# Scaled a and r of an RWKV-7 recurrence interleaved in their scratch, and its identity blocks copied on chip

## The chip, the cores and the metric

The kernel runs on one core of a Trainium2 chip. The metric is the device time of one execution in microseconds (us). The engines are TensorE (PE, matmuls and transposes), VectorE (DVE), ScalarE (ACT), GpSimd (POOL) and SyncE (SP, whose queue issues most transfers). Each engine works through its own list of instructions in order, and semaphores tie the lists together.

## What is computed

The reference is a trunk of two layers on 512 tokens of width 1024 in float32. Layer 0 mixes tokens by RWKV-7, layer 1 by a spatial gating unit, and each is followed by a SwiGLU feed-forward layer. The change lies in layer 0, in the recurrence of 16 heads of width 64:

```python
def step(S, inp):
    r_t, w_t, k_t, v_t, a_t, b_t = inp
    sa = jnp.einsum('bhij,bhj->bhi', S, a_t)
    S = (S * w_t[:, :, None, :]
         + sa[..., None] * b_t[:, :, None, :]
         + v_t[..., None] * k_t[:, :, None, :])
    y = jnp.einsum('bhij,bhj->bhi', S, r_t)
    return S, y
```

## The kernel before, in words

The recurrence isn't stepped token by token. The sequence is cut into 8 chunks of 64 tokens (C = 64, NC = 8), and what happens inside a chunk is solved for all chunks beforehand, so that only 8 short steps per head remain in sequence. The 16 heads are handled in 4 blocks b of 4 heads: in a block, q (0, 1) picks a pair of heads, and the two heads hd of a pair lie in the upper and the lower 64 partitions. hh (0, 1) picks a half of the chunks, and cc one of its 4 chunks.

The work of layer 0 is a list of steps, `PLAN` (line 33). For block b they are:

- **P**, `kr_proj`: the k and r projections. A weight unit of 512 KB comes by SP's queue (line 138), ScalarE rounds it to a high part (131), VectorE makes the low part (132), and TensorE does three products for each (`mm3`, 156 to 158).
- **E**, `early`: decay, keys and the scaled operands. `ma` is the scaled a (it lies in the buffer of tw), and r is scaled in place (656, 668). Both are written to DRAM scratch `sa` (670, 671), and k and kp to scratch `sb` (674), already interleaved by chunk. Scratch is there because the next step wants other partitions and another order. The buffers of tw and ta come from a pool of two, so ScalarE's first write to the next block's tw (619) waits until the transfer of `sa` has read the old one.
- **V**, `v_proj`: the values, in four steps of two weight units each, thus eight units of 48 products for all heads.
- **F**, `front`: loads from scratch. `ST` takes 512 KB of `sb` (682). For each of the four units (hh, q) the tile `MV` holds a and r block-diagonally by head: GpSimd clears the other half (687) and transfers bring a and r (689), n = 0 for a and 1 for r. The tile `BX` gets identity blocks by transfers from the constant `ident` (702), into `bx[head, 2 + hd]`. Then TensorE multiplies `MV` by `ST` (`lm`, 708) and transposes `ST` (`bkt`, 721). VectorE writes masked products into `MV` and `BX` (711, 716), and ScalarE fills `LA` and `BX` (714, 715, 725, 726).
- **B**, `back`: the triangular solve. VectorE transposes `LA` (734), runs 15 dependent pairs of small operations (747, 749) and transposes the result twice (752, 753). TensorE then joins the parts in a chain of small products (`Qp`, `Np`, `Tp`, `Q2p`, `T2p`, 769 to 801), `mp` (810) and `gh` (817). VectorE adds the identity blocks of `BX` to `gh` and writes the chunk operators into `MV` (819, 820). `mvt` (760) are transposes of `MV` that `mp` needs.
- **S**, `scan`: the 8 chunks in sequence: `us` (846) and `Yp` (859) on TensorE, the state update on VectorE and ScalarE (848, 851), the values by SP (831).
- **N**, `finish`: group norm, bonus and gate.

The plan is only the order in which the instructions are written. A scheduler with a timeline of its own then orders every engine's list, so any edit can move instructions far from its place. `MV`, `BX`, the split inputs `xsp` and others share one pool of 17 slots (tag s); four of the inputs of V lie there until V's last product. A `BX` copy thus waits for a slot, and so does what stands behind it on its queue. All waits of a transfer are taken on the queue that issues it, in order.

## Time and profile before

| what | value |
|---|---|
| median of 3 runs | 1393.85 us (1392.23 to 1398.0) |
| profiled execution | 1395.72 us |
| its span, first to last instruction | 1394.0 us |
| mean granted clock of TensorE | 0.971 |
| busy time of TensorE, VectorE, ScalarE, GpSimd | 1332.0, 783.9, 579.2, 152.6 us |
| transfers of `sa` into `MV` (689) | 64 of 64 KB |
| transfers of `ident` into `BX` (702) | 32 of 64 KB |
| writes of `sa` (670, 671) | 8 of 512 KB |

Rows of groups have the form "line engine operation out<-in xcount". A busy TensorE isn't TensorE at its peak: its clock is granted by a throttle, and a stretch at 0.5 takes twice the time for the same work. Rows marked SPq are issues of transfers: their time is that of the issue, not of the transfer.

### The profile page before, as it was taken

How to read it: one execution, taken by the hardware profiler on the slowest of the kernel's cores; microseconds unless marked ns; L12 is line 12 of the kernel's file. 1: busy time of each engine (PE TensorE's matmuls, PEld its weight loads, DVE VectorE, ACT ScalarE, POOL GpSimd, SP SyncE). 2: the span in 40 equal slices, each digit the busy share in tenths (PEclk: the TensorE clock that was granted, in tenths of full speed). 3: DMA queues.
4: the chain of work that ended last, by engine and by line, in shares of the span. 5: the costliest groups of instructions: out<-in, count | busy, mean ns of one | idle time of the engine just before them, and what ended most of it. 6: DMA issues, size and time to landing. Idle time of an engine off the chain costs nothing.

```text
span 1394.0 us, 21544 instructions
## 1 busy us (share of the span) xinstructions
PE 1332.0 (96%) x8512; PEld 1088.7 (78%) x8512; DVE 783.9 (56%) x1373; ACT 579.2 (42%) x1076; POOL 152.6 (11%) x190
## 2 busy tenths in 40 slices
PE   5999979989799899999999999999999999999998
PEld 3677768878687688888888887878888888888886
DVE  7975776579847565544553225575574554453223
ACT  5665765566543453222322224543463332232121
POOL 5000200111000021111110002010121111110000
PEclk8999979989799999999999999999999999999999
DMA  5145375432214233333322332342223333332231
GB/s 150 36 140 148 108 208 166 127 77 69 92 49 158 61 101 112 91 95 102 91 91 91 103 109 76 107 138 89 91 77 93 103 91 93 103 92 91 91 105 61
DMA packets 209956, 142.00 MB, mean 102 GB/s; under 512 B 59536, under 2 KB 185024, under 8 KB 209856
## 3 DMA queue, kind: packets, MB, share of 16 engines
q1 hardware_dynamic: 208560, 135.91, 33.0%
q0 software_dynamic: 1296, 4.72, 1.0%
q8 instruction: 67, 1.10, 0.3%
q14 instruction: 33, 0.27, 0.1%
HBM read 124.35 MB, written 14.16 MB: 99 GB/s over the span
## 4 chain that ended last, share of the span: by engine, by line
PE 62%; DVE 2%; ACT 0%; issue 0%; DVEq 0%
PE gu L157 12%; PE gu L158 12%; PE gu L156 11%; PE acc L157 8%; PE acc L158 8%; PE acc L156 8%; PE u L158 1%; PE u L157 1%; PE u L156 1%; DVE x L273 1%; PE s L1065 1%; PE ptr L218 0%; DVE hT L59 0%; DVE rt L208 0%; DVE ry L209 0%; DVE hn L270 0%
## 5 line engine op out<-in xcount | busy, mean ns | idle before, releaser
L131 ACT CAST whi<-wraw 128x1024 fp32r<-128x1024 f32 x177 | 185.7, 1049 | 481.3 <-PE gu L157 250.5
L132 DVE TENSOR_TENSOR wlo<-wraw,whi 128x1024 fp32r<-128x1024 f32 x177 | 263.1, 1487 | 206.3 <-ACT whi L131 202.3
L156 PE MATMUL gu<-hT,whi 128*128 128x512 f32 (+1 forms) x768 | 288.8, 378 | 1.8 <-ACT hT L57 1.7
L157 PE MATMUL gu<-hT,whi 128*128 128x512 f32 (+1 forms) x768 | 288.5, 377 | 1.1 <-DVE hT L59 1.1
L158 PE MATMUL gu<-hT,wlo 128*128 128x512 f32 (+1 forms) x768 | 289.5, 378 | 0.0
L156 PEld LDWEIGHTS gu<-hT,whi 128*128 128x128 f32 x768 | 145.0, 190 | 31.5 <-ACT hT L57 2.3
L157 PEld LDWEIGHTS gu<-hT,whi 128*128 128x128 f32 x768 | 144.9, 189 | 30.5 <-DVE hT L59 1.5
L158 PEld LDWEIGHTS gu<-hT,wlo 128*128 128x128 f32 x768 | 145.1, 189 | 28.5 <-issue 0.2
L157 PE MATMUL acc<-wlo,act 128*128 128x512 f32 x416 | 164.0, 394 | 0.0
L156 PE MATMUL acc<-whi,act 128*128 128x512 f32 x416 | 163.5, 394 | 0.0
L158 PE MATMUL acc<-whi,act 128*128 128x512 f32 x416 | 160.4, 394 | 0.0
L332 DVE TENSOR_TENSOR sg<-sg,gu 128x512 f32<-128x512 f32 x44 | 30.3, 688 | 142.2 <-PE gu L158 139.2
L333 POOL TENSOR_TENSOR sg<-sg,hn 128x512 f32<-128x512 f32 x44 | 57.0, 1295 | 417.3 <-DVE sg L332 417.3
L156 PEld LDWEIGHTS acc<-whi,act 128*128 128x128 f32 x416 | 78.2, 188 | 18.1
L158 PEld LDWEIGHTS acc<-whi,act 128*128 128x128 f32 x416 | 78.2, 188 | 18.0
L157 PEld LDWEIGHTS acc<-wlo,act 128*128 128x128 f32 x416 | 78.1, 188 | 18.0
L330 DVE TENSOR_TENSOR sg<-gu,hn 128x512 f32<-128x512 f32 x44 | 30.4, 691 | 66.5 <-PE gu L158 66.3
L131 ACT CAST act<-sg 128x512 fp32r<-128x512 f32 x52 | 32.3, 621 | 71.7 <-POOL sg L333 57.5
L156 PE MATMUL proj<-xsp,whi 128*128 128x512 f32 x128 | 51.6, 403 | 0.0
L158 PE MATMUL proj<-xsp,wlo 128*128 128x512 f32 x128 | 51.1, 401 | 0.0
L157 PE MATMUL proj<-xsp,whi 128*128 128x512 f32 x128 | 50.3, 396 | 0.2 <-DVE xsp L132 0.2
L708 PE MATMUL lm<-MV,ST 128*128 128x128 f32 x256 | 40.0, 309 | 7.0 <-ACT BX L726 3.0
(303 smaller groups left out, 2124.0 us busy)
## 6 DMA issues: line engine op xcount, KB each, us to landing
wraw<-in_ffn_w_gate_dram SPq DMA_DIRECT2D x44, 512.0 KB
wraw<-in_ffn_w_up_dram SPq DMA_DIRECT2D x44, 512.0 KB, 3.8
wraw<-in_ffn_w_down_dram SPq DMA_DIRECT2D x44, 512.0 KB, 3.7
wraw<-in_rwkv_w_rkv_dram SPq DMA_DIRECT2D x24, 512.0 KB, 3.7
wraw<-in_sgu_w_in_dram SPq DMA_DIRECT2D x16, 512.0 KB, 3.7
x<-in_x_dram SPq DMA_DIRECT2D x8, 512.0 KB, 3.2
MV<-sa SPq DMA_DIRECT2D x64, 64.0 KB, 2.5
ST<-sb SPq DMA_DIRECT2D x8, 512.0 KB
```

The source lines that it names most:

```text
L131: self.nc.scalar.copy(hi, src)
L132: self.nc.vector.tensor_tensor(lo, src, hi.bitcast(F32), op=ALU.subtract)
L156: mm(out, lhs[0], rhs[0], start=start, stop=False)
L157: mm(out, lhs[0], rhs[1], start=False, stop=False)
L158: mm(out, lhs[1], rhs[0], start=False, stop=stop)
L273: v.scalar_tensor_tensor(xts[tt][:, c], f, y[:, 0:1], xts[tt][:, c], op0=ALU.mult, op1=ALU.add)
L330: nc.vector.tensor_tensor(sg, pp[0], yb, op=ALU.mult)
L332: nc.vector.tensor_tensor(sg, sg, pp[1], op=ALU.mult)
L333: nc.gpsimd.tensor_tensor(sg, sg, yb, op=ALU.mult)
L708: mm(lm[:, cc * P:(cc + 1) * P], st[:, cc].rearrange("p n t -> p (n t)"), mv[:, :, cc, hd, :], start=True, stop=True)
L1065: mm(acc[:, tt * P:(tt + 1) * P], vt[tt][:, m * P:(m + 1) * P], wsT[:, m, :], start=True, stop=True)
```

## The change

Scratch `sa` gets the layout that `sb` has: partition, q, chunk, then a or r, then the 64 tokens. Its two writes therefore go in pieces of 64 elements (256 bytes). In `MV` the chunk index comes ahead of the a/r index, so that one transfer brings both for a head and four chunks: 4 transfers for a unit become 2. The identity blocks are copied from `ident` by GpSimd, without transfers. All reads and writes of `MV` follow the new order of its indices; sizes of products and element counts stay as they are.

```diff
-            sa = [dp.tile([2, P, 2, T], F32, name="sa") for _ in range(4)]
+            sa = [dp.tile([P, 2, NC, 2, C], F32, name="sa") for _ in range(4)]
...
-                nc.sync.dma_start(out=sa[b][0], in_=ma)
-                nc.sync.dma_start(out=sa[b][1], in_=r)
+                for n, t in enumerate((ma, r)):
+                    nc.sync.dma_start(out=sa[b][:, :, :, n, :].rearrange("p q c t -> p (q c) t"), in_=sv(t))
...
-                        mv = MV[hh, q] = s4("MV", [P, 2, 4, 2, C])
+                        mv = MV[hh, q] = s4("MV", [P, 4, 2, 2, C])
                         for hd in range(2):
                             g.memset(mv[head[1 - hd], :, :, hd], 0.0)
-                            for n in range(2):
-                                nc.sync.dma_start(out=mv[head[hd], n, :, hd],
-                                                  in_=sa[b][n, head[hd], q, 4 * hh * C:4 * hh * C + 4 * C].rearrange("p (c t) -> p c t", t=C))
+                            nc.sync.dma_start(out=mv[head[hd], :, :, hd].rearrange("p c n t -> p (c n) t"),
+                                              in_=sa[b][head[hd], q, 4 * hh:4 * hh + 4].rearrange("p c n t -> p (c n) t"))
...
-                        nc.sync.dma_start(out=bx[head[hd], 2 + hd],
-                                          in_=self.ident[head[hd], head[hd]].unsqueeze(1).broadcast_to([64, 4, C]))
+                        g.tensor_copy(bx[head[hd], 2 + hd], self.ident[head[hd], head[hd]].unsqueeze(1).broadcast_to([64, 4, C]))
...
-                            mm(lm[:, cc * P:(cc + 1) * P], st[:, cc].rearrange("p n t -> p (n t)"), mv[:, :, cc, hd, :], start=True, stop=True)
+                            mm(lm[:, cc * P:(cc + 1) * P], st[:, cc].rearrange("p n t -> p (n t)"), mv[:, cc, :, hd, :], start=True, stop=True)
...
-                        v.tensor_tensor(mv[:, 0, :, hd], gv[:, 0], bx[:, 2 + hd], op=ALU.add)
-                        v.tensor_tensor(mv[:, 1, :, hd], gv[:, 1], mv[:, 1, :, hd], op=ALU.add)
+                        v.tensor_tensor(mv[:, :, 0, hd], gv[:, 0], bx[:, 2 + hd], op=ALU.add)
+                        v.tensor_tensor(mv[:, :, 1, hd], gv[:, 1], mv[:, :, 1, hd], op=ALU.add)
```

The transposes of `MV` and the products of the scan are edited in the same way. From line 688 on the lines are one or two lower than before.

The scheduler orders the lists anew. First SP's queue before, from the first loads of `MV` to the next weights of V (the `wraw` rows of 128x4x256 are V's weight units, two `L138` issues of one row being two units):

```order
L138 DMA wraw<-in_rwkv_w_rkv_dram 128x4x256 x3
L689 DMA MV<-sa 64x4x64 x16
L702 DMA BX<-ident 64x4x64
L670 DMA sa<-tw 128x1024
L702 DMA BX<-ident 64x4x64 x5
...
L689 DMA MV<-sa 64x4x64 x15
L702 DMA BX<-ident 64x4x64 x2
L583 DMA Vd<-vev 128x2x256
L670 DMA sa<-tw 128x1024
L583 DMA Vd<-vev 128x2x256
L138 DMA wraw<-in_rwkv_w_rkv_dram 128x4x256 x2
```

The same place in SP's queue now:

```order
L138 DMA wraw<-in_rwkv_w_rkv_dram 128x4x256 x3
L688 DMA MV<-sa 64x8x64 x16
L138 DMA wraw<-in_rwkv_w_rkv_dram 128x4x256
L671 DMA sa<-tw 2048x1x64
L905 DMA g2r<-in_rwkv_g_dram 32x256 x2
L138 DMA wraw<-in_rwkv_w_rkv_dram 128x4x256
```

The 16 loads behind the first three V units now cover two blocks, and V's fourth and fifth unit follow directly, ahead of the loads of `ST`.

Second, TensorE's list before, where block 0's back begins with `Qp`, up to `Q2p` (rows `v` are the products of V; 24 of them stand between `lm` and `Np`):

```order
L708 MATMUL lm<-MV,ST 128x128 x3
L769 MATMUL Qp<-hn,LA 32x32 x64
L708 MATMUL lm<-MV,ST 128x128
L157 MATMUL v<-wlo,xsp 128x256
L158 MATMUL v<-whi,xsp 128x256
...
L778 MATMUL Np<-Qs,Dt 32x32 x32
L781 MATMUL Tp<-Dt,Qs 32x32 x64
L792 MATMUL Q2p<-Dn_1890,LA 32x32 x32
L156 MATMUL v<-whi,xsp 128x256
```

The same place in TensorE's list now, from the last products of V on (`lm` and `bkt` here are block 1's):

```order
L158 MATMUL v<-whi,xsp 128x256
L758 MATMUL mvt<-ident,MV 128x128 x8
L706 MATMUL lm<-MV,ST 128x128 x8
L719 MATMUL bkt<-ident,ST 128x128 x4
L706 MATMUL lm<-MV,ST 128x128 x8
L719 MATMUL bkt<-ident,ST 128x128 x4
L706 MATMUL lm<-MV,ST 128x128 x8
L767 MATMUL Qp<-hn,LA 32x32 x64
L719 MATMUL bkt<-ident,ST 128x128 x4
L706 MATMUL lm<-MV,ST 128x128 x4
L776 MATMUL Np<-Qs,Dt 32x32 x32
L779 MATMUL Tp<-Dt,Qs 32x32 x64
```

Before, 101 products of V stand behind block 0's `Qp` and ahead of the first scan product (`us`); now all 384 stand ahead of `Qp`, and block 1's front stands in their place. Ahead of the first `lm` stand 192 products of V now, and 144 before.

## The prediction

> **What bounds the kernel now.** I read the page first, for the engine that carries the span.

> ```profile
> PE 1332.0 (96%) x8512; PEld 1088.7 (78%) x8512; DVE 783.9 (56%) x1373; ACT 579.2 (42%) x1076; POOL 152.6 (11%) x190
> PE 62%; DVE 2%; ACT 0%; issue 0%; DVEq 0%
> ```

> TensorE (PE) is busy nearly throughout and carries the chain that ended last. So a change to transfers can only pay where TensorE waits or runs at a lowered clock. I therefore asked for the stretches of the first layer, where every changed line runs.

> ```profile
> 100.00:170.00 70.00, 70.00 (x353) 53.71 (x352) 44.27 (x55) 42.06 (x54) 8.61 (x18) 1.00 0.43 121
> 170.00:215.00 45.00, 36.21 (x254) 32.77 (x253) 32.81 (x42) 25.96 (x54) 4.32 (x9) 0.77 0.79 206
> 215.00:290.00 75.00, 69.50 (x1043) 64.85 (x1045) 48.30 (x114) 43.78 (x105) 10.19 (x24) 0.95 0.47 136
> 290.00:345.00 55.00, 50.84 (x878) 44.52 (x870) 44.11 (x106) 35.65 (x98) 6.91 (x16) 0.91 0.28 70
> 345.00:375.00 30.00, 22.53 (x452) 18.66 (x450) 25.20 (x65) 18.18 (x35) 1.22 (x4) 0.66 0.27 83
> ```

> The columns are the stretch, its length, busy PE, PE weight loads, VectorE, ScalarE, GpSimd, then the granted clock. Busy time times clock is work at full speed, and the rest is lost. From 100 to 170 us nothing is lost. In the next four stretches 45 - 36.21 x 0.77 = 17.1 us, then 9.0, 8.7 and 15.1 us are lost. The change can win back part of these 50 us and no more. The first stretch is the front of block 0. What SyncE's queue (SP) does before and in it shows why.

> ```profile
> 138.51 12.72 SPq L138 DMA_DIRECT2D wraw<-in_rwkv_w_rkv_dram  x3
> 151.34 11.03 SPq L689 DMA_DIRECT2D MV<-sa  x16
> 162.47 0.62 SPq L702 DMA_DIRECT2D BX<-ident  x1
> 169.62 3.32 SPq L702 DMA_DIRECT2D BX<-ident  x5
> 183.82 9.88 SPq L689 DMA_DIRECT2D MV<-sa  x15
> 193.75 1.29 SPq L702 DMA_DIRECT2D BX<-ident  x2
> 197.81 1.64 SPq L138 DMA_DIRECT2D wraw<-in_rwkv_w_rkv_dram  x2
> ```

> The V projection needs eight weight units of 48 products. Three are loaded before 151.3 us, and the fourth stands behind the 31 MV loads and 8 identity loads of these rows, until 197.8. What that does to TensorE shows in the V products of three stretches and in the front's own products (L708) from 186 to 215 us.

> ```profile
> 150.00:170.00 20.00, 11.09 (x80) 9.84 (x81) 0.00 (x0) 1.00 0.34 83
> 170.00:185.00 15.00, 11.20 (x67) 10.29 (x65) 1.07 (x2) 0.77 0.86 216
> 185.00:205.00 20.00, 0.50 (x2) 0.30 (x2) 0.00 (x0) 0.83 0.72 201
> L708 PE MATMUL lm<-MV,ST 128*128 128x128 f32 x64 | 11.9, 354 | 5.5 <-ACT BX L726 3.0 <-POOL Dm L696 1.5 <-POOL Dm L695 0.7
> ```

> 80 and 67 V products are the three units; then come 2 in 20 us. TensorE has only the short dependent products of the front left and waits for their evictions: 5.5 us in front of L708 alone, at 354 ns for a product whose mean over the whole run is 309.

> **The change, part by part.** *Fewer issues on SP.* A MV load brings twice as much, and the identity loads are gone.

> ```profile
> L689 SPq DMA_DIRECT2D MV<-sa x64: 573/614/1377, 151.3 to 331.6; - x64
> L702 SPq DMA_DIRECT2D BX<-ident x32: 590/614/1490, 162.5 to 348.7; - x32
> L674 SPq DMA_DIRECT2D sb<-k x8: 520/622/670, 89.9 to 202.9; - x8
> ```

> The middle figure is the median in ns of one issue. An L674 issue has four times the 256-byte pieces of an L689 issue and costs the same (622 against 614 ns), so a doubled MV load should still cost 0.61 us. With 32 + 32 issues fewer, 64 x 0.614 = 39 us of SP time go. SP is not on the path by itself; what counts is what stood behind those issues. The order of SP shown above tells it: the 16 issues at 151.3 now load MV of blocks 0 and 1 whole, and the fourth V unit comes straight behind them, at about 162.5 instead of 197.8. The buffers allow it, since it reuses the raw tile of the second unit.

> *What TensorE does with it.* By the new order 192 V products, not 144, stand ahead of the first L708, and groups of 6 to 27 of them stand between the L708 of block 0.

> ```profile
> 165.00:170.00 5.00, 5.00 (x43) 4.59 (x42) 3.49 (x4) 2.42 (x3) 0.00 (x0) 1.00 0.00 0
> L708 PE MATMUL lm<-MV,ST 128*128 128x128 f32 x256 | 40.0, 309 | 7.0 <-ACT BX L726 3.0 <-issue 1.7 <-POOL Dm L696 1.5
> L721 PE MATMUL bkt<-ident,ST 128*128 128x128 f32 x64 | 10.2, 283 | 1.8 <-ACT BX L715 1.8
> L760 PE MATMUL mvt<-ident,MV 128*128 128x128 f32 x64 | 11.8, 318 | 1.6 <-ACT MVt L763 1.6
> L158 PE MATMUL v<-whi,xsp x128: 274/282/682, 157.0 to 263.1; 128*128 128x256 f32 x128
> ```

> From 165 to 170 us TensorE did nearly nothing but V products: 5.00 / 43 = 0.116 us each. 384 - 80 = 304 are left at 170, so 35.3 us. Beside them stand block 0's L708 (40.0 / 4 = 10.0), L721 (2.6) and L760 (3.0), and some 5 us of feature products. That is 56 us, so V ends at about 227 if I allow 1 us of waiting. Now the last one starts at 263.1 (last row). Of the 17.1 us lost I take 15 as regained, because a V group of 12 to 27 (1.4 to 3.1 us) covers an eviction.

> *What is late next.* The cover that V gives here is missing in block 0's back. There the triangular solve on VectorE runs between these two rows, and TensorE waits for its end:

> ```profile
> 212.87 2.05 DVE L734 STREAM_TRANSPOSE LX<-LA 128x1024 f32<-128x1024 f32 x1 [0.77 <-ACT LA L714]
> 231.84 2.01 DVE L753 STREAM_TRANSPOSE Dt<-Dm 128x1024 f32<-128x1024 f32 x1
> L846 PE MATMUL us<-su,MV x224: 222/222/271, 263.3 to 439.9; 128*64 128x64 f32 x112
> L769 PE MATMUL Qp<-hn,LA x128: 191/191/212, 289.6 to 290.8; 32*32 32x32 f32 x128
> ```

> The solve needs all of block 0's L708. Some 46 V products, a group of L721 and L760 still follow the last of them, 9 us, so L734 starts at about 218, 5 us later than now. The solve then takes 19 us as now, to 237. From 227 to 237 TensorE has L708 and L721 of block 1, 24 x 10.0 / 32 = 7.5 and 1.3 us, so little is lost. Then the 30 us from the solve to the first scan product at 263.3 hold 101 V products by the old order (11.7 us) and none by the new (the order of TensorE above). That leaves about 18 us of bare chain: first scan product at about 255, 8 us earlier, with 4 us more of block 1's front done. Behind it block 1's solve sits on VectorE ahead of the scan's first update, so I put its L769 at 274 against 289.6, 15 us earlier; but half a front of block 2 (16 of 32 L708, 5.0 us, and some L721) and two scan chunks (about 2 us), which stand ahead of it now, come later. Net 8 us, and since those L708 later fill waits that TensorE has anyway (23.8 us are lost from 290 to 375), I take 10 us. So about 5 of the 15 us regained are given back.

> *Interleaved sa.* The eight writes go in pieces of 256 bytes instead of rows of 4 KB.

> ```profile
> sa<-r SPq DMA_DIRECT2D x4, 512.0 KB, 4.2
> sb<-k SPq DMA_DIRECT2D x8, 256.0 KB, 4.6
> sb<-kp SPq DMA_DIRECT2D x8, 256.0 KB, 6.3
>   ACT tw L619: 10.0, 3
> 89.18 0.69 ACT L619 ACTIVATE tw<-w,halfb 128x512 f32<-128x512 f32 x1 [3.79 <-DMA sa<-tw]
> 89.76 1.04 ACT L131 CAST whi<-wraw 128x1024 fp32r<-128x1024 f32 x1
> 93.55 1.22 DVE L132 TENSOR_TENSOR wlo<-wraw,whi 128x1024 fp32r<-128x1024 f32 x1
> ```

> An sa write lands in 4.2 us now. As a floor it stays there; as a ceiling it takes twice the slower half-size sb write, 12.6 us. Nearest is an sb write behind its twin, so I take 6.5 us. Behind it waits ScalarE's L619, and behind that on ScalarE a weight cast. The cast ended at 90.8 and its other half began on VectorE only at 93.55: 2.7 us of cover, and ScalarE waits there three times in all, 10.0 us together (fourth row). I cost it at 0; with the cover gone it is the slow rival. [...]

> *GpSimd copies.* No copy of 64x256 stands in the trace.

> ```profile
> L687 POOL MEMSET MV<- 64x512 f32 x32 | 16.7, 522 | 59.2 <-DVE MV L819 34.9 <-DVE xs L477 10.5 <-PE Yp L859 9.2
> L333 POOL TENSOR_TENSOR sg<-sg,hn 128x512 f32<-128x512 f32 x44 | 57.0, 1295 | 417.3 <-DVE sg L332 417.3
> ```

> Half a 64x512 memset is 0.26 us, half a two-input 128x512 product 0.65. I take 0.35, near the memset: 32 x 0.35 = 11 us on an engine that is busy 4.32 of the 45 us above. The products that read the identity (L819) run long after, so 0. A copy that waits for a slot holds the memsets queued behind it, which SP's queue did so far to its own followers; I cost that at 0 too. The changed strides of MV leave shapes and counts on TensorE and VectorE as they are: 0.

> **Sum.** Regained 15, given back 5, the rest 0: 10 us. The profiled execution took 1395.72 us (span 1394.0 and 1.72 around it), 1.87 above the median of the runs. 1395.72 - 10 = 1385.7, and in the median's frame 1383.9: I say 1384.

> **The rivals.** *It carries through* (larger gain): the half front that now lies later fills waits in 290 to 375 us, and the 15 us at block 1's solve stay whole, with some 7 of the 23.8 us lost there. 22 us, 1372. For it: VectorE and TensorE both have slack there. Against: the new order has no V products left by then.

> *All is given back* (no change). Blocks 0 and 1 then run their backs as bare as the stretch from 345 to 375 us, which has no V and loses 15.1 us. 2 + 15.1 + 15.1 = 32.2 us lost, against 17.1 + 9.0 + 8.7 = 34.8 now: 3 us gained, 1391. For it: the order of TensorE shown above. Against: block 1's L708 lie in block 0's chain.

> *The clock stays low* (no change). Of the 17.1 us, 8.8 are idle and 8.3 clock. If the low clock is not a result of the waits, only 15 - 8.3 - 5 = 2 us are gained: 1392. [...]

> *ScalarE starves the projections* (slower). If an sa write takes the 12.6 us, L619 is held 8.4 us longer in three blocks, 5.7 us beyond the 2.7 of cover, with the weight cast behind it. TensorE then waits 3 x 5.7 = 17 us from 90 to 175 us, and perhaps 4 us at a lowered clock after. Less the gain of 10 this is +11: 1405. It decides from a landing of about 7 us on. Against: DMA is busy 0.43 of 100 to 170 us, so there is room.

> **How the numbers follow.** A change under 0.5% (7 us, so from 1387 to 1401) can't be told from none here. Chances: forecast 0.44 (own range 1378 to 1390, of which 0.35 is faster and 0.09 the same), larger gain 0.17, given back 0.20, clock 0.05, slower 0.14. Faster 0.35 + 0.17 = 0.52; same 0.09 + 0.20 + 0.05 = 0.34; slower 0.14. The range leaves out the slow rival and the far side of the large gain: 1371 to 1398.

> **What would show it.** Right: the fourth V load at about 163 us; clock near 1.00 and PE busy over 95% from 170 to 215; V done by 230; first scan product at about 255; the second block's first Qp product at about 274. Wrong: waits for sa ahead of L619 over 6 us, with TensorE idle between 90 and 170; Qp as late as now; an issue of a MV load over 1 us; TensorE waiting for a GpSimd row more than the 2.2 us of now.

## The result and the profile after

The changed kernel takes 1403.67 us (median of 11 executions, 1398.5 to 1409.68) against 1395.87 beside it (11 executions, 1391.8 to 1398.0). The ratio is 1.0063, 95% interval 1.0047 to 1.0078: it is slower by 8 us, where 10 us faster had been forecast. The profiled execution of the changed kernel took 1406.98 us, with a span of 1405.3; that of before has a span of 1394.0. So the two profiles differ by 11.3 us, 3 more than the medians.

The same stretches as in the prediction, and the one behind them, from the table by stretch of the changed kernel:

```profile
170.00:215.00 45.00, 44.62 (x406) 42.44 (x405) 35.41 (x45) 30.02 (x57) 3.27 (x6) 1.00 0.83 221
215.00:290.00 75.00, 60.37 (x917) 53.21 (x916) 47.44 (x108) 36.00 (x89) 17.63 (x38) 0.75 0.31 91
290.00:345.00 55.00, 51.92 (x734) 45.64 (x731) 40.78 (x101) 39.29 (x109) 9.28 (x24) 0.94 0.21 53
345.00:375.00 30.00, 19.91 (x514) 16.82 (x512) 28.01 (x70) 16.77 (x35) 2.00 (x6) 0.66 0.27 82
375.00:490.00 115.00, 105.82 (x1143) 87.24 (x1138) 65.52 (x161) 39.96 (x91) 1.70 (x4) 0.91 0.26 84
```

The front is as forecast: TensorE is busy 44.62 of 45 us at full clock, where 17.1 us were lost before. The next row is the surprise. It lost 9.0 us before; now it loses 75 - 60.37 x 0.75 = 29.7. The last row ran at 0.98 before.

The queue of SP and the V products show that the front gained for the reason given:

```profile
151.80 11.83 SPq L688 DMA_DIRECT2D MV<-sa  x16
163.73 0.57 SPq L138 DMA_DIRECT2D wraw<-in_rwkv_w_rkv_dram  x1
...
L158 PE MATMUL v<-whi,xsp x128: 274/281/682, 157.5 to 222.4; 128*128 128x256 f32 x128
```

The fourth V unit is issued at 163.73 (before: in the issues from 197.81 on), and V ends at 222.4 instead of 263.1. What follows is best seen in steps of 10 us. First the kernel before, with V products until 263 us:

```profile
240.00:250.00 10.00, 7.08 (x138) 6.82 (x125) 2.06 (x3) 2.27 (x4) 0.00 (x0) 0.67 0.15 56
250.00:260.00 10.00, 10.00 (x137) 9.69 (x137) 2.94 (x4) 5.12 (x13) 0.00 (x0) 0.98 0.32 80
260.00:270.00 10.00, 9.48 (x84) 8.46 (x84) 5.97 (x12) 6.81 (x17) 3.12 (x6) 1.00 0.51 122
270.00:280.00 10.00, 8.74 (x90) 7.45 (x90) 8.38 (x27) 7.12 (x18) 3.31 (x8) 1.00 0.92 264
```

Then the changed kernel:

```profile
240.00:250.00 10.00, 9.13 (x275) 8.47 (x276) 3.57 (x6) 6.34 (x16) 0.73 (x2) 0.59 0.03 7
250.00:260.00 10.00, 6.13 (x87) 4.98 (x85) 7.68 (x21) 5.38 (x13) 1.21 (x4) 0.67 0.31 103
260.00:270.00 10.00, 9.46 (x50) 8.42 (x50) 9.13 (x23) 1.17 (x3) 2.51 (x5) 0.50 0.12 28
270.00:280.00 10.00, 10.00 (x57) 8.30 (x57) 2.77 (x9) 1.86 (x6) 2.56 (x6) 0.50 0.15 34
```

Read the column before the last two, the granted clock. In windows of 0.1 us both clocks fall soon after 240 us (at 243.5 before, at 241.9 now). Before, it is back at 250.3 and stays. Now it is back for 3.4 us only (252.1 to 255.6) and then stays at a half until 282.8, through 20 us in which TensorE shows almost no idle time. A busy column of 10.00 hides a loss of 5 us here: it is stretched work (16 `gh` took 3.09 us at 0.50, from 275.49, and 1.71 at 1.00, from 283.09). So the loss is mostly no wait. The longest wait in the stretch is 3.04 us, ahead of `mp`, and the clock falls for the second time during it:

```profile
257.46 2.07 PE L808 MATMUL mp<-MVt,bdT 128*128 128x128 f32 x8 [3.04 <-DVE bdT L803]
260.20 3.10 PE L815 MATMUL gh<-BX,MVt 64*128 64x128 f32 x16 [0.68 <-ACT MVt L810]
```

### The profile page after: what moved, and what is told of

Its sections match the earlier page's. It is cut to its first block, busy times and chain, and to the rows that moved or that the text cites. A ratio compares the mean times of both kernels' runs of the same rounds, so it can differ in the third digit from the quotient of the medians.

```text
span 1405.3 us, 21489 instructions
## 1 busy us (share of the span) xinstructions
PE 1337.8 (95%) x8512; PEld 1094.1 (78%) x8512; DVE 788.0 (56%) x1373; ACT 579.4 (41%) x1076; POOL 169.9 (12%) x222
## 4 chain that ended last, share of the span: by engine, by line
PE 61%; DVE 2%; ACT 0%; issue 0%; DVEq 0%
PE gu L157 11%; PE gu L158 11%; PE gu L156 11%; PE acc L157 8%; PE acc L158 8%; PE acc L156 8%; PE u L158 1%; PE u L157 1%; PE u L156 1%; DVE x L273 1%; PE s L1063 1%; DVE hT L59 0%; PE ptr L218 0%; DVE rt L208 0%; DVE ry L209 0%; DVE hn L270 0%
## 5 line engine op out<-in xcount | busy, mean ns | idle before, releaser
L131 ACT CAST whi<-wraw 128x1024 fp32r<-128x1024 f32 x177 | 185.6, 1049 | 482.4 <-PE gu L157 251.7
L132 DVE TENSOR_TENSOR wlo<-wraw,whi 128x1024 fp32r<-128x1024 f32 x177 | 263.8, 1490 | 206.6 <-ACT whi L131 202.6
L158 PE MATMUL gu<-hT,wlo 128*128 128x512 f32 (+1 forms) x768 | 289.3, 377 | 0.0
L158 PEld LDWEIGHTS gu<-hT,wlo 128*128 128x128 f32 x768 | 145.4, 190 | 28.3 <-issue 0.2
L158 PE MATMUL acc<-whi,act 128*128 128x512 f32 x416 | 160.4, 394 | 0.0
L332 DVE TENSOR_TENSOR sg<-sg,gu 128x512 f32<-128x512 f32 x44 | 30.2, 687 | 142.0 <-PE gu L158 139.0
L333 POOL TENSOR_TENSOR sg<-sg,hn 128x512 f32<-128x512 f32 x44 | 56.7, 1288 | 417.1 <-DVE sg L332 417.1
L158 PEld LDWEIGHTS acc<-whi,act 128*128 128x128 f32 x416 | 78.1, 188 | 18.1
L131 ACT CAST act<-sg 128x512 fp32r<-128x512 f32 x52 | 32.3, 621 | 72.1 <-POOL sg L333 57.9
L158 PE MATMUL proj<-xsp,wlo 128*128 128x512 f32 x128 | 51.1, 401 | 0.0
L148 POOL TENSOR_TENSOR wlo<-wraw,whi 128x1024 fp32r<-128x1024 f32 x12 | 29.0, 2418 | 138.9 <-ACT whi L147 138.9
## 6 DMA issues: line engine op xcount, KB each, us to landing
wraw<-in_ffn_w_gate_dram SPq DMA_DIRECT2D x44, 512.0 KB
wraw<-in_ffn_w_up_dram SPq DMA_DIRECT2D x44, 512.0 KB, 3.8
wraw<-in_ffn_w_down_dram SPq DMA_DIRECT2D x44, 512.0 KB, 3.7
wraw<-in_rwkv_w_rkv_dram SPq DMA_DIRECT2D x24, 512.0 KB, 3.8
wraw<-in_sgu_w_in_dram SPq DMA_DIRECT2D x16, 512.0 KB, 3.8
x<-in_x_dram SPq DMA_DIRECT2D x8, 512.0 KB, 3.3
ST<-sb SPq DMA_DIRECT2D x8, 512.0 KB, 4.1
```

What stands on the lines that cost most here:

```text
L131: self.nc.scalar.copy(hi, src)
L132: self.nc.vector.tensor_tensor(lo, src, hi.bitcast(F32), op=ALU.subtract)
L148: nc.gpsimd.tensor_tensor(lo, raw, hi.bitcast(F32), op=ALU.subtract)
L158: mm(out, lhs[1], rhs[0], start=False, stop=stop)
L332: nc.vector.tensor_tensor(sg, sg, pp[1], op=ALU.mult)
L333: nc.gpsimd.tensor_tensor(sg, sg, yb, op=ALU.mult)
```

## The experiments

All kernels are compared by what is **lost**. In steps of 2.5 us I added up idle time of TensorE and busy time x (1 - granted clock), in three ranges: the front (170 us to block 0's first Qp), block 0's back (from there to block 1's first Qp), and all from 170 us to the first product of the next layer (`gu`, at 487.7 us before and 498.9 after). The rest of each range is work at full speed. All these figures come from one profiled execution of each kernel, and its time ("profiled") isn't the median: e4, e7 and f1 were profiled in their fastest execution, f4 and h1 in their slowest. "V end" is the start of the last V product; the clock is that of 240 to 285 us. Medians stand beside a median of before on the same chip of 1395.4 to 1397.3.

| kernel | V end | clock | lost in front | in back | in all | profiled us | median us | ratio to before (95%) |
|---|---|---|---|---|---|---|---|---|
| before | 263 | 0.92 | 18.3 | 8.3 | 61.6 | 1395.7 | 1395.9 | |
| changed | 222 | 0.58 | 5.3 | 24.5 | 75.5 | 1407.0 | 1403.7 | 1.0063 (1.0047, 1.0078) |
| e1 interleaving alone | 250 | 0.96 | 9.5 | 6.3 | 60.2 | 1393.4 | 1391.3 | 0.9975 (0.9963, 0.9987) |
| e2 copies alone | 252 | 0.96 | 12.5 | 5.5 | 52.8 | 1389.6 | 1391.5 | 0.9971 (0.9957, 0.9985) |
| e3 changed, loads split | 256 | 0.96 | 16.0 | 5.9 | 61.7 | 1398.2 | 1396.4 | 1.0007 (0.9989, 1.0024) |
| e4 before, V on a queue | 242 | 0.96 | 11.1 | 6.1 | 51.2 | 1383.0 | 1390.6 | 0.9969 (0.9952, 0.9985) |
| e6 changed, 32 fills | 222 | 0.89 | 5.3 | 11.4 | 54.4 | 1393.0 | 1395.7 | 1.0003 (0.9988, 1.0018) |
| e7 changed, 12 fills | 223 | 0.81 | 5.3 | 14.5 | 54.7 | 1393.7 | 1399.2 | 1.0015 (0.9996, 1.0035) |
| e8 before, 12 fills | 264 | 0.96 | 16.7 | 5.2 | 65.9 | 1407.3 | 1407.3 | 1.0081 (1.0056, 1.0106) |
| e9 changed, 12 fills, 32 rows | 222 | 0.54 | 5.3 | 27.2 | 88.3 | 1421.3 | 1419.7 | 1.0162 (1.0140, 1.0183) |
| f1 changed, V3 held | 249 | 1.00 | 10.4 | 4.8 | 52.5 | 1389.7 | 1394.1 | 0.9989 (0.9975, 1.0002) |
| f3 f1 and block 2 filled | 251 | 0.96 | 11.0 | 6.5 | 57.4 | 1394.6 | 1397.7 | 1.0009 (0.9996, 1.0023) |
| f4 e4 and block 2 filled | 245 | 0.96 | 12.5 | 6.3 | 56.8 | 1396.3 | 1392.3 | 0.9969 (0.9952, 0.9986) |
| g1 front first | 220 | 0.93 | 6.7 | 14.2 | 65.5 | 1401.8 | 1401.4 | 1.0039 (1.0024, 1.0054) |
| h1 before, two queues | 226 | 0.62 | 9.9 | 25.5 | 86.1 | 1416.4 | 1410.2 | 1.0093 (1.0066, 1.0119) |
| h3 changed, again | 222 | 0.70 | 5.9 | 21.2 | 73.8 | 1405.3 | 1401.6 | 1.0038 (1.0016, 1.0059) |

My theory (A) was that V comes so early that block 0's back is left bare, and that the clock falls there. The rivals were GpSimd's copies (B), the interleaved scratch (C), later both together (D), and chance in the order that the scheduler writes (E).

**The parts by themselves.** e1 keeps the identity transfers, e2 keeps `sa`, its layout in `MV` and the 64 loads.

```diff
 e1: the changed kernel, but
-    g.tensor_copy(bx[head[hd], 2 + hd], self.ident[...]...)
+    nc.sync.dma_start(out=bx[head[hd], 2 + hd], in_=self.ident[...]...)
 e2: the kernel before with the opposite edit
```

> Only the interleaved sa (32 MV loads instead of 64); the identity blocks still come by 32 transfers on SP. In the order of TensorE 36 V products are left when block 0's first Qp comes (101 before, 0 after). Theory A (the early V weights take the cover from block 0's back, the granted clock falls to a half there, and the time regained in the front is lost): between the two kernels, 1397 to 1403 us, clock from 240 to 285 us about 0.7 to 0.8. Theory B (the GpSimd copies, 0.5 to 0.9 us each, hold VectorE or GpSimd): as before or faster, 1396 us or less, since no copy is there. Theory C (the interleaved writes and loads of sa cost it): as after, 1404.

> Only the identity blocks copied by GpSimd; sa and the 64 MV loads as before. 63 V products are left at block 0's first Qp. Theory A: near before, 1392 to 1398 us, clock from 240 to 285 us 0.85 or more, since the cover is mostly there. Theory B: as after, 1404. Theory C: as before or faster, 1396 or less.

Each part alone gains 4 us: it wins part of the front, V still runs to 250 us, and the back loses less than before. B falls with e2 and C with e1. Theory A was wrong on e1, in the clock (0.96) and in the time.

**V early, without the change.**

```diff
 e4: the kernel before, V's weight() gets q=g
-        nc.sync.dma_start(out=raw, in_=src)
+        (q or nc.sync).dma_start(out=raw, in_=src)
```

> The kernel before with neither part of the change; only the eight V weight units are loaded by GpSimd's queue instead of SP's, so that they no longer stand behind the MV and identity loads. 7 V products are left at block 0's first Qp. Theory A: it reproduces the loss without the change: V done before 230 us, clock about 0.6 from 240 to 285 us, 1400 to 1406 us. Theories B and C: the front's gain shows without the copies or the interleaving, 1382 to 1392 us.

This is a gain of 5 us, and theory A in that form falls: early weights don't hurt by themselves. But V ran to 242 us here, since the front still lost 11.1 us. And with only 7 V products behind block 0's first Qp the back was still covered: 16 of block 1's `lm` stood ahead of `mp` (251.05 to 254.4 us), where the changed kernel waits 3.04 us. So cover needn't be V. That led to theory A2: what costs is a sparse stretch from V's end on, after which the clock stays low. In the 35 us from 222.5 on, TensorE was busy 32.08 us before (V in them), and 23.73 in the changed kernel; the 22.5 us from 260 on follow in the second row of each. Before:

```profile
222.50:257.50 35.00, 32.08 (x647) 31.35 (x646) 18.05 (x31) 14.32 (x31) 1.12 (x2) 0.90 0.25 78
260.00:282.50 22.50, 20.71 (x204) 18.22 (x204) 16.75 (x46) 15.32 (x38) 6.42 (x14) 1.00 0.69 189
```

Changed:

```profile
222.50:257.50 35.00, 23.73 (x547) 20.32 (x545) 24.81 (x52) 22.39 (x57) 5.21 (x12) 0.83 0.32 104
260.00:282.50 22.50, 21.96 (x121) 19.00 (x123) 11.90 (x30) 4.38 (x11) 5.27 (x10) 0.50 0.13 30
```

**Both parts, SP's issues put back.**

```diff
 e3: the changed kernel, each MV load in two
-    nc.sync.dma_start(out=mv[head[hd], :, :, hd]..., in_=sa[b][head[hd], q, 4*hh:4*hh+4]...)
+    for n in range(2):
+        nc.sync.dma_start(out=mv[head[hd], :, n, hd], in_=sa[b][head[hd], q, 4*hh:4*hh+4, n])
```

> The changed kernel with each MV load split in its two halves again: GpSimd copies and interleaved sa stay, but SP has 32 issues more, and 68 V products are left at block 0's first Qp (0 in the changed kernel, 63 and 36 in the two halves of the change alone, which both took 1391). Theory A2 (the two parts cost nothing; what costs is that together they let V end at 222 us, so that TensorE's stretch from 222 to 257 us is sparse and the granted clock stays at a half from 245 to 282 us): clock over 0.85 from 240 to 285 us and 1390 to 1394 us. Rival D (copies and interleaving disturb each other, whenever V runs): 1400 to 1405. Rival E (chance in the order that the scheduler writes): anything from 1390 to 1405, with the clock no guide to it.

The clock is 0.96 as A2 expects, the time 1396.4, 2 us over its range and no different from before. D falls: copies and interleaving together cost nothing that can be told here (interval 0.9989 to 1.0024). The front kept its old loss (16.0), so nothing was gained either.

**Work without use as cover.** `fill` writes products of the constant-like tile `sg` into a bank that the next step overwrites. e6 has 6, 6, 8, 4, 4, 4 of them at Q2p, T2p and the four mp; e7, e8 and e9 only the first two sixes.

```diff
+    fill = lambda t: [mm(t, sg[:, 0, 0:P], sg[:, 0, :], start=True, stop=True) for _ in range(0 if b else 6)]
     Q2p = self.bank("pt", "Q2p")
+    fill(Q2p)
...
     T2p = self.bank("pt", "T2p")
+    fill(T2p)
 e9: sg[0:32, 0, 0:P], sg[0:32, 0, :]
```

> The changed kernel plus 32 products of 128x512 whose results are overwritten, in block 0's back ahead of Q2p (6), T2p (6) and the four mp groups (8, 4, 4, 4): about 7 us of work at full clock that computes nothing, where the V products stood before. Theory A: the granted clock from 240 to 285 us rises from 0.6 to 0.85 or more, block 1's first Qp comes no later than now (285.6 us), and the time stays at 1404 or falls to 1398, in spite of 7 us more work. Theories B and C, and any in which the clock there is only an effect: 7 us later, 1411.

> The changed kernel with 12 products of 128x512 without use (128 rows, about 2.7 us at full clock) in block 0's back, 6 ahead of Q2p and 6 ahead of T2p, and none at mp. Theory A2: a dense stretch of some 4 us there is enough to bring the clock back to 1.00 by 252 us; it then stays, the first Qp of block 1 comes at 277 to 281 us instead of 285.6, and the time is 1390 to 1396. Rival (the cover has to last through mp and gh): clock back at a half from 255 us on, 1400 to 1405. Rival E: clock as in theory A2, time not below 1400.

> The kernel before with the same 12 products without use in block 0's back. There the clock is 1.00 already from 215 to 240 us and 0.92 from 240 to 285 us. Theory A2: no gain to be had, 0 to 4 us slower than before, 1396 to 1400. If instead the added products help for another reason (they move the scheduler's order), it is faster than before by 3 us or more.

> As the 12 products without use in the changed kernel, but with 32 rows of the array instead of 128: the same time on TensorE, a quarter of the array. Theory A2 with TensorE's time as what counts: as with 128 rows, 1390 to 1396, clock 1.00 from 252 us on. If the used part of the array counts (from 260 to 282 us the changed kernel's products of 64 rows and 64 columns kept TensorE over 93% busy and the clock stayed at 0.50): the clock stays at about 0.5 until 280 us and the time at 1402 to 1408.

e6 does 32 products more than the changed kernel and is 6 to 8 us faster than its two medians; block 0's back loses 11.4 us instead of 24.5, and block 1's first Qp comes at 281.2 instead of 285.6. Its median of 1395.7 is 2 us below the range that A gave. Its steps of 5 us show how the clock comes back, with the fills from 245.92 to 251.05:

```profile
240.00:245.00 5.00, 4.62 (x145) 4.24 (x147) 1.12 (x2) 3.48 (x11) 0.11 (x1) 0.57 0.01 3
245.00:250.00 5.00, 5.00 (x146) 4.11 (x138) 1.37 (x2) 2.14 (x4) 0.00 (x0) 0.74 0.03 7
250.00:255.00 5.00, 5.00 (x88) 4.35 (x87) 1.80 (x3) 2.55 (x9) 0.00 (x0) 1.00 0.52 160
```

e9 has the same fills at the same place on a quarter of the array's rows:

```profile
240.00:245.00 5.00, 4.87 (x122) 4.25 (x122) 1.12 (x2) 3.31 (x11) 0.27 (x1) 0.50 0.01 3
245.00:250.00 5.00, 5.00 (x138) 3.88 (x131) 1.37 (x2) 1.98 (x4) 0.00 (x0) 0.50 0.01 3
250.00:255.00 5.00, 5.00 (x51) 3.88 (x46) 0.70 (x1) 0.58 (x1) 0.00 (x0) 0.50 0.33 108
```

TensorE is as busy, but the clock comes back only at 256.9, where in e6 it was back at 247.5. e9 is 20 us slower than e7, and 12 over the range of its slower expectation. In e7 the clock had not fallen when the fills began, so its trace can't show them bringing it back. It fell later, at mp and gh:

```profile
240.00:245.00 5.00, 3.93 (x190) 3.46 (x192) 1.77 (x4) 4.29 (x14) 1.00 (x2) 1.00 0.02 3
245.00:250.00 5.00, 4.79 (x113) 3.76 (x103) 2.07 (x3) 2.21 (x4) 0.00 (x0) 1.00 0.05 10
250.00:255.00 5.00, 3.82 (x85) 3.06 (x83) 2.10 (x2) 2.94 (x8) 0.00 (x0) 1.00 0.63 206
255.00:260.00 5.00, 2.73 (x11) 2.44 (x12) 4.52 (x16) 2.60 (x5) 1.22 (x4) 0.64 0.00 0
260.00:265.00 5.00, 5.00 (x29) 4.43 (x29) 3.57 (x13) 0.12 (x1) 1.05 (x2) 0.50 0.03 6
```

e7 lies between its two expectations: block 1's first Qp comes at 280.5, as A2 said, but the median of 1399.2 is over A2's range. So twelve fills were too few to keep the clock up through mp and gh.

e8 went wrong: A2 allowed 0 to 4 us, and it is 11.5 slower. Up to block 2's first Qp it is level with before (342.5 against 342.4 us); from there to block 3's it takes 57.4 us against 48.6, in a list that the scheduler had ordered anew: 6.6 us more work stands in that stretch, 3.6 more are lost to the clock and 1.4 less to waits. So rival E is real and can be worth 9 us in one stretch.

**Cover without added work.** The changed kernel, with the split of V3's two weight units made to wait for block 0's LX (`gate` is 1.0):

```diff
 back, b == 0:
+    v.tensor_scalar(one, LX[:, 0, 0:1], 0.0, 1.0, op0=ALU.mult, op1=ALU.add)
 weight, for V3:
-    nc.scalar.copy(hi, raw)
+    nc.scalar.activation(hi, raw, AF.Copy, scale=gate[:, 0:1])
```

> The changed kernel with one V group of four held back: the split of V3's two weight units waits for block 0's LX (218 us), by a factor of 1.0 that is worked out from LX. Both parts of the change stay, no work is added. 31 V products are left at block 0's first Qp and V runs to about 250 us (222 in the changed kernel). Theory A2: the front keeps most of its gain (5 to 9 us lost from 170 us to the first Qp, 5.3 in the changed kernel and 18.3 before), block 0's back loses 5 to 8 us instead of 24.5, the clock is over 0.85 from 240 to 285 us, and the time is 1383 to 1391, faster than both kernels. If copies and interleaving together cost by themselves, or if the order of the later blocks decides: 1397 or more.

```profile
170.00:215.00 45.00, 41.55 (x358) 38.08 (x356) 33.38 (x44) 29.97 (x61) 4.31 (x8) 0.96 0.88 221
...
240.00:285.00 45.00, 38.84 (x753) 34.73 (x753) 31.01 (x73) 30.19 (x80) 12.14 (x28) 1.00 0.41 104
```

The back loses 4.8 us, and the median is 7.5 to 9.5 below the changed kernel's two, with every edit of the change in place. But it is 3 us over A2's range, and can't be told from before (interval 0.9975 to 1.0002). The profiled execution (1389.7) lies inside the range, so its trace doesn't show what the others lost. In it the front gave back part of its gain (10.4 us lost).

**The same cover for block 2; the front first.** f3 and f4 add the 12 fills for `b == 2` to f1 and e4. g1 changes the plan.

> As with V3 held back, and 12 products without use (128 rows, 128x512) in block 2's back ahead of Q2p and T2p, where every kernel so far ran at 0.5 to 0.8 from 345 to 375 us and lost 11.5 to 22.8 us between the third and the fourth block's first Qp. Theory A2 carried over: the clock comes back 10 us earlier there and 2 to 5 us are gained beyond V3 held back. Against: VectorE is busy 25 to 28 of those 30 us with two solves, so that TensorE waits whatever its clock; then it is 0 to 3 us slower.

> The kernel before with V's weights on GpSimd's queue (1390.6, clock 0.50 from 340 to 360 us) and the same 12 products in block 2's back. As for V3 held back with these products: 2 to 5 us faster than 1390.6 if the clock decides there, 0 to 3 us slower if VectorE's two solves do.

```diff
 g1
-PLAN = "P0 E0 P1 P2 E1 P3 E2 E3 X0 F0 B0 F1 ..."
+PLAN = "P0 E0 P1 E1 P2 E2 P3 F0 E3 X0 B0 F1 ..."
```

> The changed kernel with a plan that puts the projections of the last block behind the early work of the block before it and block 0's front ahead of the last early step (P0 E0 P1 E1 P2 E2 P3 F0 E3 X0 B0 and on as before). By the order of TensorE block 0's front runs among the first 190 V products, and the other 192 stand in one piece during the solve on VectorE; none is left behind block 0's first Qp. Theory A2: what counts is whether the stretch ahead of the back is dense; here it is up to the first Qp, so the clock is 1.00 when the back begins, and the time is 1380 to 1392. If the cover has to last into the back itself: clock 0.5 to 0.7 in the 45 us after the first Qp, and 1395 to 1405.

The fills in block 2 bring nothing: f3 is 3.6 us slower than f1, and f4 has e4's ratio to before, 0.9969. Between the third and the fourth block's first Qp, f4's trace loses 2.3 us less to the clock than e4's and 4.0 more to waits; f3's loses no less to the clock than f1's (8.2 against 7.2). That VectorE's two solves decide there fits f4, but isn't shown.

g1 is slower than before and 9 us over A2's range. It didn't bring about what it was meant to test: V ended at 219.8 us, 8 us ahead of the first Qp, from 215 to 240 us TensorE was busy only 13.94 of 25 us, and the clock fell at 225.4. In the 45 us behind Qp it was 0.84, above what the other reading gave, whose time came true. g1 loses more to waits than to the clock in its back (8.5 against 6.0 us).

**The loss without any edit of the change.**

```diff
 h1: the kernel before, transfers and layouts kept
-    nc.sync.dma_start(out=mv[head[hd], n, :, hd], ...)
+    (g if n else nc.sync).dma_start(out=mv[head[hd], n, :, hd], ...)
-    nc.sync.dma_start(out=bx[head[hd], 2 + hd], ...)
+    g.dma_start(out=bx[head[hd], 2 + hd], ...)
```

> The kernel before, with every transfer and layout as it was, but the 32 identity transfers and the second half of the 64 MV loads issued from GpSimd's queue instead of SP's: SP has 64 issues less, as in the changed kernel, without a copy on GpSimd and without an interleaved sa. By the order of TensorE all V products stand ahead of block 0's first Qp, and from there to T2p the order is that of the changed kernel (Qp 64, bkt 4, lm 4, Np 32, Tp 64, Q2p 32, lm 4, bkt 4, T2p 32). Theory A2: V ends at 220 to 228 us, the clock from 240 to 285 us is 0.5 to 0.75, and the kernel is slower than before by 3 to 10 us (1399 to 1406). If copies or interleaving are needed for the loss: 1383 to 1394.

> The changed kernel once more, beside the run on two queues, for its spread: 1398 to 1409 us. Theory A2: its executions differ by how long the clock stays low, so that time falls as the mean granted clock of an execution rises (1398.5 us at 0.973 and 1409.7 at 0.964 in the first eleven); 12 more should lie on the same line, about 1.2 us per 0.001. Without such a tie the spread has another cause.

h1's two stretches, to be read against those of the changed kernel above:

```profile
222.50:257.50 35.00, 26.09 (x581) 23.15 (x579) 24.32 (x52) 23.47 (x59) 9.16 (x18) 0.90 0.40 124
260.00:282.50 22.50, 21.77 (x116) 18.80 (x116) 15.07 (x43) 3.97 (x9) 6.05 (x11) 0.50 0.11 27
```

V ends at 226.5, TensorE's list from Qp to T2p is the changed kernel's, and the half clock and the loss are there (25.5 us in the back, 1410 us, more than expected), with no copy on GpSimd and no interleaving. Why it is slower than the changed kernel isn't told; its front lost 9.9 us. The changed kernel's own executions fit too: in the first eleven the time falls by 0.96 us for each 0.001 of mean granted clock (correlation -0.84), in the twelve of h3 by 1.24 (-0.78). Its clock from 240 to 285 us was 0.58 in one profiled execution and 0.70 in the other.

## Why the prediction was wrong

**Right: the front.** The fourth V unit at 163.73 (said 162.5), V's end at 222.4 (227), clock 1.00 and TensorE 99% busy, LX at 217.75 (218), Qp at 236.7 (237). Of the 17.1 us lost from 170 to 215 us, 15 were to be regained, and 17.1 - 0.4 = 16.7 were; up to the first Qp it is 18.3 - 5.3 = 13.0, as waits came up behind V's end.

**Right: the costs put at 0.** ScalarE's L619 waited 8.3 us for `sa` (10.0 before). The writes of r into `sa`, taken at 6.5 us, landed in 4.7 (4.2 before). The copies took 559 ns in the mean instead of 350, and e2 and e3 show that this costs nothing that can be told:

```profile
  ACT tw L619: 8.3, 3
...
sa<-r SPq DMA_DIRECT2D x4, 512.0 KB, 4.7
...
L701 POOL COPY BX<-ident 64x256 f32<-64x256 f32 x32 | 17.9, 559 | 46.8 <-PE Yp L857 22.5 <-PE us L844 9.4 <-PE v L158 9.3
```

Two writes of r show their landing in the trace of before, 5.1 and 3.4 us after their issue in rows of 4 KB; one shows it in the changed kernel's, 4.7 us in pieces of 256 bytes. So a cost of the smaller pieces isn't shown here.

**Wrong: "about 18 us of bare chain" and "about 5 of the 15 us regained are given back".** This is the step that failed. The order was read rightly (no V behind Qp, 101 products before), but the bare chain was costed at the pace that it had under V's cover, where the clock was at a half for 6.8 of 30 us (243.5 to 250.3). First scan product at 255, block 1's Qp at 274 were said; 263.2 and 285.6 came. From the first Qp to the first scan product it took 26.5 us instead of 18, with the clock at a half from 241.9 to 252.1 and again from 255.6. Behind the first Qp the changed kernel loses 24.5 - 8.3 = 16.2 us more in block 0's back, 14 of them clock, and 10.8 more from there to `gu`: 27.0 in place of 5. 13.0 - 27.0 = -14; it has 2.7 us less work in the range, and `gu` is 11.2 us late.

**The rivals.** "All is given back" named the mechanism, but took 15.1 us for each bare back and ended at 1391. "The clock stays low" doubted the clock at the place where it recovered (1.00 from 170 to 215 us). "ScalarE starves" had nearly the time (1405) with a cause that did not happen: TensorE was busy 70.00 of the 70 us up to 170, at 1.00.

**Open.** How much of the 10.8 us behind block 0 is chance of the order (E: 9 us in e8) and how much follows from the late start isn't told apart. What in an execution decides how long the clock stays low is known in part. In the 16 profiled executions it changed between 170 and 290 us only on steps of 3.41 us (last section), and these lay elsewhere in each. In the first trace of the changed kernel the wait of 2.19 us ahead of `bkt` lies inside one step, and the clock falls at its end, 241.9. In h3 a step ends inside the same wait, at 239.5 (four steps ahead of the fall at 253.1), and the clock holds until 253.1. That is two traces, and no run changed this alone.

## What to carry to other kernels

Work that an earlier transfer lets run early is taken from where it stood as cover, so cost that later place with the clock that the barest stretch of the same profile shows (here 0.66 from 345 to 375 us), not with 1.00: after the event, 18 us at 0.66 make 27, and 26.5 came. A stretch with TensorE "busy" all the time may be at half clock (here 270 to 280 us: busy 10.00 of 10 us, clock 0.50): read busy time and granted clock together, and sum both as lost time. Freeing a queue can be right and still need one thing more, a tie that keeps some independent products for the bare stretch (f1: 7.5 us or more below the changed kernel for one dependence, though no faster than before for certain). The fastest kernels here (1391, 0.3% below before) took half of the change (e1, e2) or moved only V's weights to another queue (e4).
